# A fused two-block transformer kernel: the pool of feature tiles is allocated from the other end of the on-chip memory

## The chip, the cores and the metric

The kernel runs on one core of one Trainium2 chip. The core has a matrix engine (TensorE, PE in the profile; its weight loads are PEld), a vector engine (DVE), a scalar engine (ACT), a general engine (GpSimd, POOL), queues that issue transfers (SP and POOL here), 16 DMA engines, and two on-chip memories of 128 partitions: SBUF, which holds operands, and PSUM, into which TensorE accumulates. The metric is the device time of one execution in microseconds (us), as the median of several runs.

## The reference

The input is 512 tokens of width 1024, all in float32. A first block runs once: RMS norm, one projection `x @ w_in`, a recurrent mixer (RWKV-7) and a sparse attention (NSA) side by side, `h + y @ w_out`, RMS norm, and a gated feed-forward network of hidden width 2816:

```
def swiglu(x, w_gate, w_up, w_down):
    return (jax.nn.silu(x @ w_gate) * (x @ w_up)) @ w_down
```

A second block runs twice, with a layer norm ahead: a projection, a depthwise convolution, a differential attention with four heads and an attention to a memory of 256 tokens, an output projection, a layer norm, and a feed-forward network of hidden width 4096:

```
x = layer_norm(ALPHA * x + mixed, ln1_g[l], ln1_b[l])
ff = jnp.square(jax.nn.relu(x @ w_up[l])) @ w_down[l]
x = layer_norm(ALPHA * x + ff, ln2_g[l], ln2_b[l])
```

## The kernel before

Every large product is done in split precision. An operand is held as a high part (`xh`, `wh`, `hh`), rounded to TensorE's float32r, and a low part (`xl`, `wl`, `hl`), the rest. `mm3` (line 212) makes one product of a 128-row slice out of three matmuls: high by low, low by high, high by high, all into one PSUM tile (`acc`). In a matmul the first operand after the output is stationary (loaded into the array by a weight load), the second is moving (streamed through it, 512 columns, 256 in a few places). In a row of the profile, `acc<-xl,wh` names the moving operand first.

There are two shapes of large product.

- **Feature-major** (`fm_part`, line 230, and `fm_steps`, line 235): weights are stationary, features `X` are moving. One output tile of 128 features by 512 tokens takes 8 slices x 3 = 24 matmuls. It makes the gate and up products of both feed-forward networks and the projections at the start of the mixers. `gemm_fm_lead` (line 249) does the first four tiles of a stage in two halves of 256 tokens, so that they can begin before all tokens are ready.
- **Token-major** (`gemm_tm`, line 263): hidden activations (or mixer outputs) are stationary, weights are moving. It makes the down products and `w_out`.

```
def fm_part(ps, wt, X, t0, t1):
    wh, wl = wt
    for k in range(8):
        mm3(ps[:, t0:t1], wh[:, k, :], wl[:, k, :], *xk(X, k, slice(t0, t1)), k == 0, k == 7)
```

A weight tile of 512 KB arrives by DMA in `wraw` (or in halves of a feature tile, `raws`), ACT rounds it to `wh` (line 204) and DVE or POOL subtracts to get `wl` (line 208). The weights of the second block's mixers are split ahead of time during the feed-forward networks (`split_ahead`, line 152: `ahead` tiles, written back to HBM as `split`).

SBUF is divided into pools. `scope` (line 71) opens a pool; `side="right"` allocates it from the top of SBUF downwards, otherwise it is allocated from the bottom upwards, each pool behind the ones that are open. The pool of feature tiles, `xp` (line 78, name "x"), has 8 buffers of 8192 bytes a partition. It stays open for the whole kernel and holds `X`, the mixer outputs `y`, `qm`, `kt`, `vt2`, the memory's features `mh` and `ml`, `ahead` and `raws`. It is opened third of the SBUF pools, after `const` and `small`, so the pools that are opened later on the left lie above it. In the first stage the weights and several work pools are taken from the right (lines 369 to 372, and line 1119 for the first part of `w_out`); from line 1192 on the weight pool is on the left.

The order of instructions on each engine is set by a scheduler that works from the program's dependences, except where a stretch is pinned to the written order (`P["pin"]`).

Of the kernel before, what the change touches and what calls it, by code (L numbers as in the profile page):

```python
# [8 lines left out]
F32 = mybir.dt.float32  # L9
# [41 lines left out]
def tile_hybrid_blocks(ctx: ExitStack, tc: tile.TileContext, I, out):  # L51
# [19 lines left out]
    def scope(st, name, bufs=1, **kw):  # L71
        return st.enter_context(tc.tile_pool(name=name, bufs=bufs, reuse_waits="tile", **kw))
# [2 lines left out]
    small = ctx.enter_context(tc.tile_pool(name="small", bufs=8))  # L75
    wk = ctx.enter_context(tc.tile_pool(name="wk", bufs=1, space=PSUM))
    dram = ctx.enter_context(tc.tile_pool(name="dram", bufs=1, space=DRAM))
    xp = scope(ctx, "x", 8)

    ka = const.tile([128, 483], F32, name="ka")  # L80
    ident, mhalf, tri, hones = ka[:, 0:128], ka[:, 128:160], ka[:, 160:288], ka[:, 288:290]
# [1732 lines left out]
```

## Time and profile before

| | us |
|---|---|
| median of 3 runs (1955.12 to 1959.68) | 1959.52 |
| the profiled execution, whole | 1963.28 |
| its span, first to last instruction | 1961.3 |
| TensorE busy in the span | 1915.7 (98%) |
| DVE busy | 1132.1 (58%) |
| ACT busy | 782.9 (40%) |
| mean granted TensorE clock | 0.993 of full |

A busy TensorE is not the same as a TensorE at its peak: matmuls overlap, and their ends are modelled. What a stream of matmuls costs is read from the starts of successive ones in the timeline.

### The profile page before, as it was taken

What the parts mean: (1) busy time and instruction counts of PE and PEld (TensorE: products, weight loads), DVE (VectorE), ACT (ScalarE), POOL (GpSimd) and SP (SyncE); (2) the same over time, 40 slices, a digit from 0 to 9 for tenths busy, and PEclk for the clock granted to TensorE, in tenths of its full rate; (3) what the DMA queues carried; (4) which work ended last, traced back from release to release, by engine and by line L of the source; (5) the groups of instructions that cost most, each with busy time, mean ns of one, the idle gap of its engine ahead of it and who ended that gap; (6) DMA issues with size and microseconds to landing.
All of it is one profiled execution on the core that took longest, in us unless ns stands there. A gap on an engine that the chain in (4) does not pass through costs nothing.

```text
span 1961.3 us, 27788 instructions
## 1 busy us (share of the span) xinstructions
PE 1915.7 (98%) x10831; PEld 1583.3 (81%) x10831; DVE 1132.1 (58%) x1976; ACT 782.9 (40%) x1419; POOL 382.2 (19%) x450
## 2 busy tenths in 40 slices
PE   8999999999999999999999999999999999999998
PEld 7777777798888888978888888888978888888886
DVE  4674667665455535668766565545668764434345
ACT  4523565434434322356615444331357523223230
POOL 2211132223322101432112232100442010000000
PEclk9899999999999999999999999999999999999999
DMA  6147100458999922833448999732743433323331
GB/s 170 44 127 177 32 2 2 132 160 292 344 345 323 296 86 70 309 136 117 148 141 287 336 354 350 258 107 81 279 149 101 144 119 107 104 90 97 97 97 43
DMA packets 231591, 326.24 MB, mean 166 GB/s; under 512 B 29813, under 2 KB 157151, under 8 KB 231460
## 3 DMA queue, kind: packets, MB, share of 16 engines
q1 hardware_dynamic: 197636, 200.86, 33.2%
q0 software_dynamic: 33824, 123.62, 17.8%
q8 instruction: 85, 1.39, 0.3%
q14 instruction: 46, 0.38, 0.1%
HBM read 249.44 MB, written 77.09 MB: 166 GB/s over the span
## 4 chain that ended last, share of the span: by engine, by line
PE 88%; DVE 6%; ACT 2%; DMA 1%; issue 1%; POOL 1%; SPq 0%; DVEq 0%; ACTq 0%; POOLq 0%
PE acc L63 74%; PE ps_s L63 2%; PE ps_t L63 2%; PE ps_pt L63 1%; PE ps_po L63 1%; PE ps_pv L63 1%; PE ps_q L63 1%; DMA wraw<-in_w_in_dram 1%; PE ps_g L63 1%; PE ps_y L63 1%; PE ps_pm L63 1%; DVE e L1502 1%; ACT pr L1565 1%; DVE cv L1402 0%; PE ps_ptb L63 0%
## 5 line engine op out<-in xcount | busy, mean ns | idle before, releaser
L63 PE MATMUL acc<-xl,wh 128*128 128x512 f32 (+1 forms) x1432 | 529.1, 370 | 0.3 <-DVE xl L334 0.3
L63 PE MATMUL acc<-xh,wl 128*128 128x512 f32 (+1 forms) x1432 | 524.0, 366 | 0.7 <-DVE wl L208 0.6
L63 PE MATMUL acc<-xh,wh 128*128 128x512 f32 (+1 forms) x1432 | 523.1, 366 | 0.0
L63 PEld LDWEIGHTS acc<-xl,wh 128*128 128x128 f32 x1432 | 271.0, 189 | 52.9 <-issue 3.8
L63 PEld LDWEIGHTS acc<-xh,wh 128*128 128x128 f32 x1432 | 270.8, 189 | 48.2
L63 PEld LDWEIGHTS acc<-xh,wl 128*128 128x128 f32 x1432 | 270.7, 189 | 47.1 <-DVE wl L208 1.3
L63 PE MATMUL acc<-wh,hl 128*128 128x512 f32 x688 | 267.8, 389 | 0.0
L63 PE MATMUL acc<-wh,hh 128*128 128x512 f32 x688 | 266.8, 389 | 0.0
L63 PE MATMUL acc<-wl,hh 128*128 128x512 f32 x688 | 266.6, 390 | 0.0
L204 ACT CAST wh<-wraw 128x1024 fp32r<-128x1024 f32 (+2 forms) x123 | 126.2, 1028 | 215.0 <-PE acc L63 152.1
L208 DVE TENSOR_TENSOR wl<-wraw,wh 128x1024 fp32r<-128x1024 f32 (+2 forms) x119 | 142.7, 1200 | 90.0 <-ACT wh L204 89.7
L208 DVE TENSOR_TENSOR wl<-raws,wh 128x1024 fp32r<-128x1024 f32 (+1 forms) x92 | 111.3, 1213 | 134.5 <-ACT wh L204 134.5
L296 POOL TENSOR_TENSOR r<-v,ka 128x1 f32<-128x1 f32 (+1 forms) x40 | 41.0, 1026 | 666.0 <-DVE v L315 480.2
L204 ACT CAST wh<-raws 128x1024 fp32r<-128x1024 f32 (+1 forms) x92 | 94.9, 1035 | 153.3 <-PE acc L63 114.1
L63 PEld LDWEIGHTS acc<-wh,hl 128*128 128x128 f32 x688 | 129.2, 188 | 27.0
L63 PEld LDWEIGHTS acc<-wl,hh 128*128 128x128 f32 x688 | 129.1, 188 | 26.8
L63 PEld LDWEIGHTS acc<-wh,hh 128*128 128x128 f32 x688 | 129.2, 188 | 26.8
L1769 DVE TENSOR_TENSOR h<-h 128x512 f32<-128x512 f32 x64 | 44.3, 692 | 131.2 <-ACT h L1768 130.7
L170 DVE TENSOR_TENSOR ahead<-ahead 128x1024 fp32r<-128x1024 f32 x68 | 82.5, 1222 | 62.0 <-ACT ahead L169 61.9
L169 ACT CAST ahead<-ahead 128x1024 fp32r<-128x1024 f32 x68 | 71.1, 1050 | 92.7 <-DMA ahead<-in_w_in_dram 53.5
L1768 ACT ACTIVATE h<-acc 128x512 f32<-128x512 f32 x64 | 38.2, 597 | 171.9 <-PE acc L63 171.9
L1410 POOL TENSOR_TENSOR cv<-cv,cm 128x512 f32<-128x512 f32 x60 | 89.1, 1486 | 73.2 <-ACT cm L1407 69.5
(400 smaller groups left out, 2907.8 us busy)
## 6 DMA issues: line engine op xcount, KB each, us to landing
split<-ahead POOLq DMA_DIRECT2D x136, 512.0 KB, 6.9
wh<-split SPq DMA_DIRECT2D x68, 512.0 KB, 5.5
wl<-split SPq DMA_DIRECT2D x68, 512.0 KB
ahead<-in_w_in_dram POOLq DMA_DIRECT2D x36, 512.0 KB, 7.5
wraw<-in_w_down_dram SPq DMA_DIRECT2D x32, 512.0 KB, 3.7
raws<-in_w_down_dram SPq DMA_DIRECT2D x32, 512.0 KB
wraw<-in_w_up_dram SPq DMA_DIRECT2D x28, 512.0 KB, 5.3
raws<-in_w_up_dram SPq DMA_DIRECT2D x28, 512.0 KB
```

The lines of the kernel that those rows point to most:

```text
L63: i = getattr(self.eng, op)(*a, **k)
L169: act.copy(hi.bitcast(F32R), raw)
L170: dve.tensor_sub(raw.bitcast(F32R), raw, hi)
L204: act.copy(wh, raw)
L208: P["lo"].tensor_sub(wl[:, c], raw[:, c], wh[:, c].bitcast(F32))
L296: pool.tensor_tensor(o, v, mhalf[:, :n], op=OP.pow)
L1410: pool.tensor_add(cv[f], cv[f], m)
L1502: dve.tensor_tensor_reduce(e_, ps, W[:, 384 - 128 * qt:896 - 128 * qt], -0.125, 3e38, OP.add, OP.min, nm)
L1565: act.activation(pr[:, j, :], ps[:, j, :], AF.Exp, bias=nm[:, j:j + 1], scale=0.125, accum_out=u.sums[:, j, e:e + 1])
L1768: act.activation(h, ps, AF.Relu)
L1769: dve.tensor_mul(h, h, h)
```

## The change

```
     dram = ctx.enter_context(tc.tile_pool(name="dram", bufs=1, space=DRAM))
-    xp = scope(ctx, "x", 8)
+    scope(ctx, "gap", side="right").tile([128, 24], F32, name="gap")
+    xp = scope(ctx, "x", 8, side="right")
```

A tile of 24 floats (96 bytes a partition) that nothing reads or writes is taken from the top of SBUF, and the pool of features directly below it. The pools on the left start 65536 bytes lower, the other pools on the right 65632 bytes lower. In the built programs every engine has the same instructions in the same order, with the same waits on the same counts; only addresses differ. Byte offsets in a partition, as the two programs place the tiles:

| tiles | before | after | before mod 128 | after mod 128 |
|---|---|---|---|---|
| features (8 tiles of 8192) | 21056 to 86591 | 163712 to 229247 | 64 | 0 |
| weights `wh`, `wl`, from line 1192 on | 137856 to 178815 | 72320 to 113279 | 0 | 0 |
| weights `wraw`, from line 1192 on | 129664 to 137855 | 64128 to 72319 | 0 | 0 |
| hidden activations `hh`, `hl` | 178816 to 219775 | 113280 to 154239 | 0 | 0 |
| weights `wh`, `wl`, first stage, right | from 180192 | from 114560 | 96 | 0 |
| `w_out`'s first half, right | from 204768 | from 139136 | 96 | 0 |
| residual rows `tok` | from 86592 | from 21056 | 64 | 64 |
| tiles of line 1162 (`uc`, `W`, `cvh` and others) | from 102976 | from 37440 | 64 | 64 |
| `ks` of the first block | 108096 | 42560 | 64 | 64 |

Slices of these tiles that matmuls read begin at multiples of 512 bytes from a tile's start, so the remainders hold for them too (in `vtk_steps`, line 579, whose rows have 1120 bytes, every second slice is 96 bytes further).

## Rows read from the trace of the kernel before

**Rows 1.** The page, part 1 (busy us) and part 4 (the chain).
```profile
PE 1915.7 (98%) x10831; PEld 1583.3 (81%) x10831; DVE 1132.1 (58%) x1976; ACT 782.9 (40%) x1419; POOL 382.2 (19%) x450
...
PE 88%; DVE 6%; ACT 2%; DMA 1%; issue 1%; POOL 1%; SPq 0%; DVEq 0%; ACTq 0%; POOLq 0%
```

**Rows 2.** The chain in order of time, its longest pieces: start, us, what.
```profile
463.90 204.89 PE acc L63 x888
...
1028.24 253.94 PE acc L63 x1152
...
1608.35 345.11 PE acc L63 x1560
```

**Rows 3.** Busy time by stretch: engines in the header's order, then clock, DMA share.
```profile
core 0: us, PE busy (x) PEld busy (x) DVE busy (x) ACT busy (x) POOL busy (x), PEclk, DMA share, GB/s
50.00:100.00 50.00, 48.23 (x288) 36.58 (x288) 34.83 (x54) 26.46 (x41) 14.59 (x12) 0.90 0.15 43
...
440.00:640.00 200.00, 200.00 (x872) 162.21 (x871) 103.73 (x107) 84.92 (x98) 59.79 (x96) 1.00 0.96 326
...
840.00:1000.00 160.00, 153.68 (x840) 128.23 (x839) 111.52 (x281) 91.15 (x226) 39.35 (x34) 1.00 0.35 119
...
1060.00:1200.00 140.00, 140.00 (x613) 114.50 (x612) 77.36 (x81) 57.87 (x67) 42.21 (x67) 1.00 1.02 345
1620.00:1900.00 280.00, 280.00 (x1229) 228.41 (x1228) 113.84 (x131) 81.53 (x107) 0.00 (x0) 1.00 0.32 98
```

**Rows 4.** Timeline of PE, first feed-forward network, gate and up: starts 24 matmuls apart.
```profile
570.33 0.39 PE L63 MATMUL acc<-xl,wh 128*128 128x512 f32 x1
...
575.93 0.39 PE L63 MATMUL acc<-xl,wh 128*128 128x512 f32 x1
```

**Rows 5.** Timeline of PE, the same network's down product: starts 24 matmuls apart.
```profile
539.89 0.39 PE L63 MATMUL acc<-wl,hh 128*128 128x512 f32 x1
...
545.33 0.39 PE L63 MATMUL acc<-wl,hh 128*128 128x512 f32 x1
```

**Rows 6.** Timeline of PE, last feed-forward network, up: starts 24 matmuls apart.
```profile
1864.95 0.39 PE L63 MATMUL acc<-xl,wh 128*128 128x512 f32 x1
...
1870.55 0.39 PE L63 MATMUL acc<-xl,wh 128*128 128x512 f32 x1
```

**Rows 7.** Timeline of PE, w_out: weights on the right to 392.47, on the left after.
```profile
387.09 0.39 PE L63 MATMUL acc<-wl,yh 128*128 128x512 f32 x1
...
392.71 0.40 PE L63 MATMUL acc<-wl,yh 128*128 128x512 f32 x1
...
393.41 0.39 PE L63 MATMUL acc<-wl,yh 128*128 128x512 f32 x1
...
398.90 0.39 PE L63 MATMUL acc<-wl,yh 128*128 128x512 f32 x1
```

**Rows 8.** Groups by line and form: xcount, busy us, mean ns, idle before.
```profile
L63 PE MATMUL acc<-xl,wh 128*128 128x512 f32 x1048 | 419.9, 401 | 0.0
...
L208 DVE TENSOR_TENSOR wl<-wraw,wh 128x1024 fp32r<-128x1024 f32 x113 | 138.3, 1225 | 84.3 <-ACT wh L204 84.0
...
L208 DVE TENSOR_TENSOR wl<-raws,wh 128x1024 fp32r<-128x1024 f32 x90 | 110.0, 1224 | 131.3 <-ACT wh L204 131.3
L63 PE MATMUL acc<-xl,wh 128*128 128x256 f32 x384 | 109.2, 286 | 0.3 <-DVE xl L334 0.3
```

**Rows 9.** Timeline of PE, half tiles: before the first network; memory's keys, first layer.
```profile
423.20 0.28 PE L63 MATMUL acc<-xh,wh 128*128 128x256 f32 x1
...
426.02 0.28 PE L63 MATMUL acc<-xh,wh 128*128 128x256 f32 x1
...
812.90 0.28 PE L63 MATMUL acc<-ml,wh 128*128 128x256 f32 x1
...
815.62 0.28 PE L63 MATMUL acc<-ml,wh 128*128 128x256 f32 x1
```

**Rows 10.** Waits, 1620 to 1900 us, then 1060 to 1200: total us, times, longest.
```profile
ACT wh L204 <- PE acc L63: 102.2, 24, 8.5
...
ACT wh L204 <- PE acc L63: 17.1, 9, 5.3
```

## The prediction

> **What bounds the kernel now.** I read the page first, then the chain of waits, then the busy time by stretch, then single matmuls in the timeline. TensorE is busy 98% of the span, and 88% of the chain that ends last is TensorE [rows 1]. The long pieces of the chain are unbroken TensorE work: 204.89, 253.94 and 345.11 us [rows 2], in all 804 us. In the feed-forward stretches TensorE is busy 200.00 of 200, 140.00 of 140 and 280.00 of 280 us, at a granted clock of 1.00 (2.4 GHz) [rows 3]. So there only what a matmul costs from start to start counts, and a change that touches no instruction can matter only through that. The durations in the rows (0.39 us) overlap; the cost is the distance between starts.
>
> **The instructions.** Every engine has the same instructions in the same order, with the same waits. The gap tile is read and written by nothing: 0 us. So there is no wait to add or remove and no queue that anything is moved past. What changes is addresses.
>
> **What an address costs TensorE.** The gate and up products run 24 matmuls in 575.93 - 570.33 = 5.60 us, 233.3 ns each [rows 4]. The down product, also of 512 columns, at the same granted clock and with TensorE never idle, runs 24 in 545.33 - 539.89 = 5.44 us, 226.7 ns each [rows 5]. The difference is 6.67 ns for a matmul. Three things differ between the two: which operand is moving (features there, weights here), how many matmuls follow each other into one PSUM tile (24 or 6), and where the moving operand begins (64 bytes past a multiple of 128, or on one).
>
> One product separates these. `w_out` runs with the same stationary operand and in the same order, first with weights on the right, 96 bytes past a multiple of 128, then with weights on the left, on one: 24 matmuls in 392.71 - 387.09 = 5.62 us (234.2 ns), then in 398.90 - 393.41 = 5.49 us (228.8 ns) [rows 7]. Role and grouping are unchanged, only the moving address changed, and 5.4 ns of the 6.7 went. The 2.1 ns that remain above 226.7 go with a stationary operand (`yh`, `yl`) that still begins at remainder 64. I take the rule from this: a 512-column matmul costs 226.7 ns where both operands begin on a multiple of 128 bytes, 6.7 ns more where the moving one does not, some 2 ns more where only the stationary one does not. It is a reading of four streams, not a known law.
>
> The trace differs here from the notes. The Trainium skill, page "TensorE: Matmul & The Clock Gate", section "Back-to-back issue gap", gives N / 2.4 + 2.5 ns, 215.8 for 512 columns, with no term for an address; by it the two streams would run alike and the sum would be 0. The page "SBUF — State Buffer" of the Trainium skill, section "Specifications (TRN2)", gives lines of 16 bytes; 21056 and 163712 are both multiples of 16, so by it too the sum would be 0.
>
> After the change the features begin at remainder 0, and the weights and hidden activations keep it.
>
> **The sum.** There are 3 x 1048 = 3144 matmuls of 512 columns with features moving [rows 8].
> - Feed-forward networks: the first has 22 tiles for gate and 22 for up, less 4 that run in halves: 40 x 24 = 960. The other two have 28 each outside the halves: 56 x 24 = 1344. The memory queries `qm` add 4 x 24 = 96. These 2400 stand in unbroken TensorE work: 2400 x 6.67 ns = 16.0 us, all on the path.
> - The heads' projections: 16 x 24 = 384, inside the mixers, where TensorE is busy 153.68 of 160 us [rows 3] and its gaps wait for DVE and ACT. Worth 0 to 2.6 us; I take half, 1.3.
> - The first stage: the remaining 360, 0 to 2.4 us. Here a stretch shows 48.23 busy of 50 us at a clock of 0.90 [rows 3]; I take half, 1.2.
> - Half tiles: 3 x 384 = 1152 matmuls of 256 columns [rows 8]. Before the first network they cost (426.02 - 423.20) / 24 = 117.5 ns, but the memory's keys, also at remainder 64, cost (815.62 - 812.90) / 24 = 113.3 ns [rows 9]. So at this width two rates occur at the same remainder and the rule is not enough. Bounds: 0 and 1152 x 4.2 ns = 4.8 us; I take 2, as some already run at the lower rate.
> - Stationary operands in the pool: 96 matmuls of `w_out` with weights on the right go from 234.2 to 226.7 ns, 0.7 us; another 480 (96 of `w_out`, 192 of `v_steps`, 192 of the second block's `w_out` with `y`) lose 2.1 ns, 1.0 us. Part lies in the mixers: 1.2 of 1.7.
> - Scores with `kt` moving: 128 x 6.67 ns, 0 to 0.85 us; 0.4.
> - DVE and ACT: subtractions from `raws` (remainder 64) take 1224 ns, from `wraw` (remainder 0) 1225 ns [rows 8]: 0.
>
> Together 16.0 + 1.3 + 1.2 + 2 + 1.2 + 0.4 = 22.1 us, between 16.0 and 28.4. The profiled execution took 1963.28 us, so it would take 1941.2. It lay 3.8 us above the median of the runs, 1959.52; I take the difference over to the median: 1937.4, say **1937**, with 1931 to 1943.5 as the bounds, and 2 us at each side for runs that spread over 4.6 us.
>
> **What keeps the gain from being seen elsewhere.** Faster up products ask for weights 3% sooner. In the last network ACT waits 102.2 us for TensorE to free a weight buffer [rows 10], with a DMA share of 0.32 [rows 3]: supply is far ahead.
>
> **Rivals.**
> - *Transfers become the bound.* From 440 to 640 and from 1060 to 1200 us the DMA engines are at 0.96 and 1.02 of their time [rows 3], loading weights and moving the `ahead` tiles. If these stretches kept their length, at most their 872 + 613 matmuls x 6.67 ns = 9.9 us would be lost: 1947. For it: there is no DMA time left. Against it: TensorE does not wait there now, ACT still waits for TensorE [rows 10], and the `ahead` work can end later.
> - *The rate belongs to the product, not to the address.* Then nothing changes: 1959.5. For it: the grouping into PSUM differs too, and the half tiles show two rates at one remainder [rows 9]. Against it: `w_out` [rows 7]. The two pages' rules give this time as well.
> - *Slower: the rate belongs to the region.* Moving operands between 21056 and 86591, and those from 204768 on, are the slow ones; the weights at 137856 to 178815 are the fast ones. After the change the weights lie at 72320 to 113279 and most features above 180000. If place decides, the features stay slow and the down products (86 slices x 8 x 3 = 2064 matmuls) go to 233.3 ns: +13.8 us, 1973. It decides from the point where the down product's 24 starts take 5.60 us. Against it: in the last network a quarter of the moving operands are in the tile at 78400, and the rate is the same 233.3 ns as with tiles at 21056 to 53823 [rows 4, 6]; the region would need two borders that happen to follow the remainder.
> - *The change does not do what it says.* The addresses above are the built program's, so I give this nothing.
>
> **How the numbers follow.** The forecast 0.74, transfers 0.08, no change 0.11, slower by region 0.06, and 0.01 for another gain. A difference below 0.3% (5.9 us) can't be told from none. Faster by more: 0.74 + 0.08 + 0.01 = 0.83; within: 0.11; slower: 0.06. The range 1929 to 1947 takes in the forecast's bounds with the spread of runs and the case of transfers, about 0.8.
>
> **What would show it.** In the timeline of after, 24 starts of the up products 5.44 us apart instead of 5.60 in all three networks, the down products still 5.44, and both halves of `w_out` at 5.44 to 5.46. The long pieces of the chain shorten by the count of their up matmuls times 6.67 ns, and mixers by little. Up products that stay at 5.60 us make the prediction wrong as a whole; 5.44 there with new TensorE waits for `wl` or `wraw` would be the transfers; down products at 5.60 would be the region.

## The result, and the profile after

The changed kernel took 1947.43 us (median of 4 runs, 1945.12 to 1948.87), the kernel before 1959.60; the ratio is 0.9937, 95% interval 0.9917 to 0.9956. The sign was right, the size was not: 12.2 us where 22.5 had been forecast, and 0.4 us outside the range. Measured a second time, later, the same kernel took 1944.23 against 1959.47: 0.9916 (0.9904 to 0.9928), 15.2 us.

The page of the changed kernel, its parts 1 and 4, reads almost as in [rows 1]:

```profile
PE 1899.4 (98%) x10831; PEld 1587.9 (82%) x10831; DVE 1131.4 (58%) x1976; ACT 783.3 (40%) x1419; POOL 382.4 (20%) x450
...
PE 87%; DVE 7%; ACT 3%; issue 1%; DMA 1%; POOL 1%; SPq 0%; DVEq 0%; POOLq 0%; ACTq 0%
```

The count of matmuls is the same; the busy time of TensorE fell by 16.3 us, and that of DVE, ACT and POOL moved by less than 1 us. The long pieces of the chain (start, us, what) answer to [rows 2]:

```profile
461.92 201.38 PE acc L63 x888
...
1021.43 251.00 PE acc L63 x1152
...
1597.17 340.83 PE acc L63 x1560
```

They are 3.5, 2.9 and 4.3 us shorter, with the same number of matmuls in each. The timeline of TensorE shows where that comes from: starts 24 matmuls apart, first in the down product of the first network, then in its gate and up products [rows 5, 4].

```profile
535.74 0.39 PE L63 MATMUL acc<-wh,hh 128*128 128x512 f32 x1
...
541.18 0.39 PE L63 MATMUL acc<-wh,hh 128*128 128x512 f32 x1
...
564.98 0.39 PE L63 MATMUL acc<-xh,wh 128*128 128x512 f32 x1
...
570.42 0.39 PE L63 MATMUL acc<-xh,wh 128*128 128x512 f32 x1
```

Both take 5.44 us. Before, the down product took 5.44 and the up products 5.60. `w_out`, weights on the right and then on the left [rows 7]:

```profile
384.81 0.39 PE L63 MATMUL acc<-wh,yh 128*128 128x512 f32 x1
...
390.26 0.39 PE L63 MATMUL acc<-wh,yh 128*128 128x512 f32 x1
...
392.30 0.39 PE L63 MATMUL acc<-wh,yh 128*128 128x512 f32 x1
...
397.74 0.39 PE L63 MATMUL acc<-wh,yh 128*128 128x512 f32 x1
```

They take 5.45 and 5.44 us instead of 5.62 and 5.49. So every stream of 512 columns that the prediction named runs as it said. The half tiles of 256 columns do not; before the first network:

```profile
421.28 0.28 PE L63 MATMUL acc<-xl,wh 128*128 128x256 f32 x1
...
424.16 0.28 PE L63 MATMUL acc<-xl,wh 128*128 128x256 f32 x1
```

24 of them take 2.88 us, 120.0 ns each, more than either rate of before, 117.5 and 113.3 [rows 9]. They became slower in every stretch from 417 us on. Only the 192 of the first stage kept their time, because they had taken 120.0 ns before the change too (start, us, what, starts 24 matmuls apart in the kernel before):

```profile
31.05 0.28 PE L63 MATMUL acc<-xl,wh 128*128 128x256 f32 x1
...
33.93 0.28 PE L63 MATMUL acc<-xl,wh 128*128 128x256 f32 x1
```

Transfers took nothing back: busy time by stretch, where the DMA engines are full [rows 3].

```profile
core 0: us, PE busy (x) PEld busy (x) DVE busy (x) ACT busy (x) POOL busy (x), PEclk, DMA share, GB/s
...
440.00:640.00 200.00, 200.00 (x884) 165.50 (x883) 104.24 (x106) 84.22 (x97) 61.78 (x98) 1.00 0.97 332
...
1060.00:1200.00 140.00, 140.00 (x619) 115.78 (x618) 80.34 (x85) 60.31 (x70) 42.49 (x68) 1.00 1.03 352
```

In the same time TensorE does 884 and 619 matmuls instead of 872 and 613, still without a gap, and the DMA engines move 332 and 352 GB/s instead of 326 and 345.

Since both kernels have the same instructions in the same order on TensorE, the distance from each start to the next can be subtracted, matmul by matmul. These are the sums over the two profiled executions:

| matmuls | count | gain, us | the prediction's term |
|---|---|---|---|
| 512 columns, features moving | 3144 | 19.85 | 16.0 + 1.3 + 1.2 = 18.5 |
| 256 columns, features moving | 1152 | -2.94 | +2 |
| 256 columns, memory's keys and values | 192 | -0.85 | none |
| `w_out`, `v_steps`, `cvh` (stationary in the pool, or beside it) | 864 | -0.16 | 1.2 |
| down products | 2063 | 0.15 | 0 |
| scores with `kt` moving | 128 | 0.50 | 0.4 |
| all other | 3287 | -0.98 | 0 |
| sum | | 15.56 | 22.1 |

Of the 19.85 us in the first row, 1.5 are not the address. They come from the one tile of the first stage that runs behind the small `ps_x` matmuls: in the execution of before TensorE's granted clock was 0.54 over the 3.5 us shown, so at its lower level of 1.2 GHz for most of them, and starts lay 0.43 us apart; in the execution of after, behind the same small matmuls, it was 1.00 (the engines' busy time and instructions in the order of [rows 3], then clock, DMA share and GB/s; before, then after):

```profile
187.50:191.00 3.50, 3.50 (x13) 2.70 (x10) 0.43 (x2) 0.93 (x2) 1.31 (x3) 0.54 0.35 136
```

```profile
186.50:190.00 3.50, 3.50 (x21) 2.86 (x16) 0.43 (x2) 1.15 (x2) 1.64 (x3) 1.00 0.12 43
```

So 18.3 us are left for the address at 512 columns.

### The profile page after: what moved, and what is told of

Read it like the earlier page. It is cut to its first block, busy times and chain, and to the rows that moved or that the text cites. A ratio compares the mean times of both kernels' runs of the same rounds, so it can differ in the third digit from the quotient of the medians.

```text
span 1945.9 us, 27788 instructions
## 1 busy us (share of the span) xinstructions
PE 1899.4 (98%) x10831; PEld 1587.9 (82%) x10831; DVE 1131.4 (58%) x1976; ACT 783.3 (40%) x1419; POOL 382.4 (20%) x450
## 4 chain that ended last, share of the span: by engine, by line
PE 87%; DVE 7%; ACT 3%; issue 1%; DMA 1%; POOL 1%; SPq 0%; DVEq 0%; POOLq 0%; ACTq 0%
PE acc L63 73%; PE ps_s L63 2%; PE ps_t L63 2%; PE ps_pt L63 1%; PE ps_pv L63 1%; PE ps_po L63 1%; DVE e L1503 1%; PE ps_g L63 1%; PE ps_q L63 1%; PE ps_y L63 1%; PE ps_pm L63 1%; DMA wraw<-in_w_in_dram 1%; ACT pr L1566 1%; DVE cv L1403 1%; POOL r L297 0%
```

## The experiments

Up to here the rule of the prediction (the moving operand's own remainder modulo 128) holds for 512 columns and is silent on 256. The first three runs were made to try that rule against its rival, the place in SBUF.

**The features aligned, but left where they were.** A gap of 64 bytes below the pool and one above it:

```
+    scope(ctx, "gap").tile([128, 16], F32, name="gap")
     xp = scope(ctx, "x", 8)
+    scope(ctx, "gap2").tile([128, 16], F32, name="gap2")
```

> The features stay at their old place on the left; a tile of 64 bytes below them and one above move them to remainder 0 of 128 (21120 on), and everything above them by 128 bytes, so that no other remainder changes. Theory A, the remainder decides: 24 up matmuls of 512 columns take 5.44 us as in the changed kernel, the half tiles of 256 columns 120.0 ns a matmul, and the whole takes the changed kernel's time, 1947.4 us, within 3. Theory B, the place in SBUF decides: 5.60 us, half tiles at 113 to 118 ns, 1959.5 us within 3.

Measured: 1961.96 us against 1960.56, ratio 1.0009 (0.9999 to 1.0019). TensorE's timeline in the last network's up products, starts 24 matmuls apart:

```profile
1860.19 0.39 PE L63 MATMUL acc<-xl,wh 128*128 128x512 f32 x1
...
1865.79 0.39 PE L63 MATMUL acc<-xl,wh 128*128 128x512 f32 x1
```

5.60 us, as before the change, though the features now begin on a multiple of 128 bytes, like the weights. The rule of the prediction is false. The half tiles from 408 us on took 118.3 to 120.1 ns, mostly 118.4 to 119.0, which neither theory had expected.

**The features moved, but not aligned.** The change with a gap of 32 bytes instead of 96:

```
-    scope(ctx, "gap", side="right").tile([128, 24], F32, name="gap")
+    scope(ctx, "gap", side="right").tile([128, 8], F32, name="gap")
```

> The pool of features on the right as in the changed kernel, but below a gap of 32 bytes instead of 96, so that it begins at 163776, remainder 64 as before; the first stage's weights go to remainder 64 with it. Theory A, the remainder decides: 24 up matmuls take 5.60 us, the half tiles 113.3 or 117.8 ns a matmul, 1959.5 us within 3. Theory B, the place decides: 5.44 us, and 1947.4 us within 3.

Measured: 1949.96 us, ratio 0.9947 (0.9931 to 0.9964), with the features at remainder 64. The same timeline:

```profile
1852.93 0.39 PE L63 MATMUL acc<-xh,wl 128*128 128x512 f32 x1
...
1858.42 0.39 PE L63 MATMUL acc<-xh,wl 128*128 128x512 f32 x1
```

5.49 us, 228.8 ns a matmul: neither 5.44 nor 5.60. Both runs spoke for the place against the remainder, but that value did not fit it, and in this kernel `w_out` with weights on the left had become slower than before (233.2 ns instead of 228.8).

**Streams by themselves**, for 16 pairs of remainders.

> No product of the reference: only streams of matmuls in the order of the three-matmul product, 48 of them for each pair of remainders (moving, stationary) out of 0, 32, 64 and 96 at 512 and at 256 columns, on constant data, output zeros. A letter stands for a remainder: a is 0, b 32, c 64, d 96, e 16; the first letter is the moving operand's. Theory A, remainders alone decide: 512 columns 226.7 ns at a_a, 233.3 at c_a and c_d, 228 to 230 at a_c; 256 columns 120.0 at a_a and c_d, 113.3 or 117.8 at c_a and a_c. If only the difference of the two remainders counted, a_a, b_b, c_c and d_d would be equal at either width, and a_c equal to c_a. If it is something else in the kernel (transfers, evictions of PSUM), the streams, which have neither, all take the same time, 226.7 or less at 512 columns and 113.3 at 256.

First rows of neighbouring streams of 48 matmuls, from the timeline:

```profile
60.86 0.39 PE L47 MATMUL full_a_a<-xl,wh 128*128 128x512 f32 x1
71.95 0.39 PE L47 MATMUL full_a_b<-xl,wh 128*128 128x512 f32 x1
83.04 0.40 PE L47 MATMUL full_a_c<-xl,wh 128*128 128x512 f32 x1
94.23 0.39 PE L47 MATMUL full_a_d<-xl,wh 128*128 128x512 f32 x1
```

(71.95 - 60.86) / 48 = 231.0 ns with both operands at remainder 0, where 226.7 was expected; `full_c_c` took 231.0 too, `full_a_c` 233.1. So the streams do differ with nothing else running, and not by one operand's remainder. The run, a single execution, settles no more than that: its tiles were 16512 and 4224 bytes long, so `xl` began 128 bytes further than `xh` modulo 256, and `wl` than `wh`, and every stream mixed two cases.

That flaw gave the next theory. If the cost depends on the distance from the moving operand to the stationary one modulo 256, all rates seen so far fall into line: 0 in the down products of every kernel and in the changed kernel's up products (226.7 ns), 64 in the up products before (233.3), 128 with the features aligned in place (233.3), 192 with the gap of 32 bytes (228.8). `w_out` before has 96 with weights on the right (234.2) and 192 with weights on the left (228.8).

**Streams by distance.** All four tiles begin alike modulo 256; 16 distances at two widths, and some of them with both operands shifted.

> No product of the reference: only streams of 48 matmuls in the order of the three-matmul product, on constant data, output zeros. All four operand tiles begin alike modulo 256, and a stream's letter says how far, modulo 256, the stationary operand begins behind the moving one, in steps of 16 bytes (a 0, e 64, i 128, m 192). The streams called moved (and movedhalf) shift both operands by 64, 128 and 192 (first letter) at distances 0, 64, 128 and 192 (second letter). Theory C, formed from the first runs: a matmul's cost depends on that distance modulo 256 and on nothing else of the addresses. It expects at 512 columns 226.7 ns at 0, 233 at 64 and 128, 229 at 192, the same in the shifted streams; at 256 columns 120.0 at 0, 113.3 or 117.8 at 64, 118 to 120 at 128, 117.8 at 192. Theory B, the place in SBUF: all streams lie close together, so no stream differs from another of its width. Theory A, each operand's own remainder modulo 128: a and i alike, and streams shifted by 64 unlike those that aren't.

The first rows of some streams, from the timeline; a stream's matmul costs the distance to the next stream's first row, divided by 48:

```profile
59.67 0.39 PE L47 MATMUL full_a<-xl,wh 128*128 128x512 f32 x1
70.55 0.39 PE L47 MATMUL full_b<-xl,wh 128*128 128x512 f32 x1
...
103.83 0.39 PE L47 MATMUL full_e<-xl,wh 128*128 128x512 f32 x1
115.02 0.39 PE L47 MATMUL full_f<-xl,wh 128*128 128x512 f32 x1
...
148.58 0.40 PE L47 MATMUL full_i<-xl,wh 128*128 128x512 f32 x1
159.78 0.39 PE L47 MATMUL full_j<-xl,wh 128*128 128x512 f32 x1
...
193.21 0.39 PE L47 MATMUL full_m<-xl,wh 128*128 128x512 f32 x1
204.20 0.40 PE L47 MATMUL full_n<-xl,wh 128*128 128x512 f32 x1
...
237.50 0.28 PE L47 MATMUL half_a<-xl,wh 128*128 128x256 f32 x1
243.25 0.28 PE L47 MATMUL half_b<-xl,wh 128*128 128x256 f32 x1
...
260.26 0.28 PE L47 MATMUL half_e<-xl,wh 128*128 128x256 f32 x1
265.71 0.28 PE L47 MATMUL half_f<-xl,wh 128*128 128x256 f32 x1
```

| distance, bytes mod 256 | 0 | 16 | 32 | 48 | 64 | 80 | 96 | 112 |
|---|---|---|---|---|---|---|---|---|
| 512 columns, ns | 226.7 | 226.9 | 233.1 | 233.3 | 233.1 | 231.7 | 234.2 | 233.3 |
| 256 columns, ns | 119.8 | 118.3 | 118.3 | 117.7 | 113.5 | 118.5 | 119.0 | 119.8 |

| distance, bytes mod 256 | 128 | 144 | 160 | 176 | 192 | 208 | 224 | 240 |
|---|---|---|---|---|---|---|---|---|
| 512 columns, ns | 233.3 | 233.3 | 233.3 | 229.8 | 229.0 | 233.3 | 233.3 | 227.1 |
| 256 columns, ns | 118.5 | 120.0 | 120.0 | 118.1 | 113.5 | 116.7 | 116.7 | 119.6 |

At 512 columns the theory's four values come out, and shifting both operands by 64, 128 or 192 bytes leaves them within 1 ns. At 256 columns 0 is one of the dearest distances, and 64 and 192 are the cheapest, at 113.5, where 117.8 had been expected at 192; with both operands shifted by 64, 128 or 192 bytes these two ran at 117.8, while three repeats of the unshifted stream at 64, at the end of the run, took 113.7 again. So at distances 64 and 192 a stream of 256 columns has two rates, as the kernel before already showed at distance 64 [rows 9], and the theory's second half, that nothing else of the addresses counts, is false at this width.

Nor does the table give the time of the run before it, matmul by matmul. There the three matmuls of a product have different distances, and the mean of their values in the table is right for `full_a_a` (distances 128, 128, 0: 231.1, measured 231.0) but not for `full_a_c` (192, 192, 64: 230.4, measured 233.1). The table is shown for streams in which all matmuls have one distance, as in the large products of the kernel.

The Trainium skill, page "TensorE: Matmul & The Clock Gate", section "Back-to-back issue gap", has N / 2.4 + 2.5 ns, 215.8 at 512 columns, for a matmul by itself. No stream here reaches it: the least is 226.7, and the distance between the operands, which the formula doesn't have, adds up to 7.5 ns.

**In the kernel: place against distance.** Two kernels in which the theories say the opposite. First the features moved and at remainder 0 of 128, but at distance 128 (a gap of 224 bytes):

```
-    scope(ctx, "gap", side="right").tile([128, 24], F32, name="gap")
+    scope(ctx, "gap", side="right").tile([128, 56], F32, name="gap")
```

> The pool of features on the right as in the changed kernel, below a gap of 224 bytes: it begins at 163584, remainder 0 of 128 as in the changed kernel, but from the moving features to the stationary weights (72320 on) the distance is 128 modulo 256 instead of 0. Theory C, the distance: up matmuls of 512 columns at 233 ns, half tiles at 118 to 120, the first stage alone at the lower rate (its weights move along, distance 0); about 1959 us, within 3. Theory B, the place: 226.7 to 229 ns and 1947 to 1950 us.

Measured: 1959.61 us, ratio 0.9997 (0.9988 to 1.0006): the whole gain is gone. Up products of the last network, 5.60 us for 24:

```profile
1864.69 0.39 PE L63 MATMUL acc<-xl,wh 128*128 128x512 f32 x1
...
1870.29 0.39 PE L63 MATMUL acc<-xl,wh 128*128 128x512 f32 x1
```

Then the features at their old place at distance 0 (64 bytes below the pool, 192 above):

```
+    scope(ctx, "gap").tile([128, 16], F32, name="gap")
     xp = scope(ctx, "x", 8)
+    scope(ctx, "gap2").tile([128, 48], F32, name="gap2")
```

> The features stay on the left (21120 on), 64 bytes are put below them and 192 above, so that the distance to the weights from line 1192 on (138112 on) is 0 modulo 256. Theory C, the distance: up matmuls 226.7 ns, half tiles 120.0, as in the changed kernel but for the first stage (distance 96, 234 ns): 1948 to 1952 us. Theory B, the place: 233.3 ns and 1959 to 1962 us, as in the run with 64 bytes on either side.

Measured: 1945.34 us, ratio 0.9919 (0.9905 to 0.9932), below the range of the expectation, and 5.44 us for 24:

```profile
1855.14 0.39 PE L63 MATMUL acc<-xl,wh 128*128 128x512 f32 x1
...
1860.58 0.39 PE L63 MATMUL acc<-xl,wh 128*128 128x512 f32 x1
```

The gain needs no move to the other end; 256 bytes of gaps do it. With that the place is out, and at 512 columns the distance is shown to set the rate. By what mechanism it does, no run here shows.

**The change once more.**

> The changed kernel once more, in the same rounds as the kernel before. If the spread of single runs follows the granted clock of the first stage, the ratio holds, 0.993 to 0.995 at equal clocks, and the time goes down with the mean clock by about 1.3 us for 0.001.

Measured: 1944.23 us, ratio 0.9916. Its granted clocks were 0.993 to 0.997, those of the first measurement 0.994 to 0.995. The profiled executions show where the clock differs, in the stretch from 60 to 120 us (TensorE busy and matmuls, clock, DMA share, GB/s), first in the first measurement, then in this one:

```profile
60.00:120.00 60.00, 57.01 (x356) 0.91 0.25 66
```

```profile
60.00:120.00 60.00, 55.92 (x372) 1.00 0.31 75
```

The same kernel, the same stretch of the first stage: at a clock of 0.91 it did 356 matmuls, at 1.00 372, and the two spans are 1945.9 and 1940.0 us. In the 104 runs of these kernels whose mean clock is known, one slope fitted for all falls by 1.56 us for each 0.001 of it (1.00 is 2.4 GHz). Brought to a clock of 0.995, the kernel before takes 1960.3 us (43 runs, standard error 0.2) and the changed one 1946.0 and 1945.5 (0.5 each). At equal clock the change is worth 14.3 to 14.8 us, a ratio of 0.9925 to 0.9927, just under the 0.993 to 0.995 expected. The kernel with gaps of 64 and 192 bytes is at 1946.6 by the same slope, 0.6 to 1.1 us above the changed one; its first stage ran at 234 ns in the median, the changed kernel's at 227.

**The half tiles at distance 64, all else at 0.** Weight tiles are made 256 bytes longer, and those of the half tiles and of the memory's products begin 64 bytes in (`P["off"]` is 16 around them, `P["pad"]` 64 from line 1192 on); the memory's values, where the weights are moving, come to 192 by this. The room comes from smaller buffers in the second block's mixers (`"e": 4`, `"jk": 1`).

```
+    def w_tile(n, a, b):
+        o = P["off"] if P["pad"] else 0
+        t = P["w"].tile([128, a * b + P["pad"]], F32R, name=n, tag=n)
+        return t[:, o:o + a * b].rearrange("p (a b) -> p a b", a=a)
```

> The changed kernel, in which the weight tiles from line 1192 on are 256 bytes longer and those of the half tiles and of the memory's keys and values begin 64 bytes into theirs, so that these 256-column products run at distance 64 and all others still at 0. To make room, the second block's mixers have four buffers for e instead of five and one for jk instead of two. Theory C, the distance: 960 matmuls with features moving and 192 with the memory's go from 120.0 ns to 113.3 or 117.8, 2.5 to 7.7 us less than the changed kernel's 1944.2 in its second measurement, 1936.5 to 1941.7, unless the smaller buffers cost something in the mixers. Its rival, that 256 columns are slow for a reason that only goes along with the distance (the shorter time for a weight load): they stay at 120 ns, and 1944 us or more.

Measured: 1942.66 us, ratio 0.9906 (0.9891 to 0.9921). Two of its stretches of half tiles, 24 matmuls each:

```profile
423.62 0.28 PE L63 MATMUL acc<-xl,wh 128*128 128x256 f32 x1
...
426.45 0.28 PE L63 MATMUL acc<-xh,wh 128*128 128x256 f32 x1
...
1014.86 0.28 PE L63 MATMUL acc<-xl,wh 128*128 128x256 f32 x1
...
1017.58 0.28 PE L63 MATMUL acc<-xl,wh 128*128 128x256 f32 x1
```

The first takes 2.83 / 24 = 117.9 ns, the second 2.72 / 24 = 113.3. So both rates occur again at one distance. The time is 1.0 us above the expected range.

> As the run before it, with two buffers for the mixers' l tiles instead of three, in place of four for e. The same 113.3 or 117.8 ns in the half tiles; 1936.5 to 1941.7 us if the smaller buffers cost nothing.

Measured: 1945.98 us, ratio 0.9921 (0.9906 to 0.9937), at a low mean clock (0.9935); 1943.4 brought to 0.995, above the expected range either way. The half tiles run at 113.3 to 118.0 ns.

The control, the first of these with the half tiles' weights at offset 0 again:

> The first of these three (four buffers for e, one for jk, weight tiles 256 bytes longer), with the half tiles' weights at the beginning of their tiles: distance 0 for all. It shows what the smaller buffers cost by themselves: half tiles at 120.0 ns, and the changed kernel's 1944.2 us plus that cost.

Measured: 1944.38 us, ratio 0.9914 (0.9899 to 0.9930), half tiles at 120.0 ns:

```profile
421.80 0.28 PE L63 MATMUL acc<-xl,wh 128*128 128x256 f32 x1
...
424.68 0.28 PE L63 MATMUL acc<-xh,wh 128*128 128x256 f32 x1
```

(2.88 us for 24 starts.) So the smaller buffers cost nothing that shows, and the offset brings 1.7 us between the medians, 2.9 at equal clock (1941.9 against 1944.8). In the traces the 256-column matmuls after 380 us take 135.86 us in all instead of 139.28, 3.4 less. The version is the fastest of all here, by an amount that the ratios' intervals don't separate from the changed kernel.

## Why the prediction was wrong

**What held.** In the feed-forward stretches TensorE alone sets the time; waits and transfers don't enter. The 512-column term, 18.5 us, measured 18.3 without the 1.5 that a tile gained by the clock. Within it, the first stage gave 0.9 us where 1.2 had been taken (2.38 with that tile, which would have looked like all of its 2.4), and the mixers 2.29 where 1.3 and the 0.6 of `qm` had. The up products went to 5.44 us, the down products stayed there, and no new wait for weights came up.

**The step that failed: the rule taken from `w_out`.** The prediction said that in `w_out` "only the moving address changed", and put the difference down to the moving operand's remainder modulo 128 [rows 7]. But when one operand moves, its distance to the other changes too: 96 modulo 256 in the first half, 192 in the second. The runs showed that the distance decides at 512 columns and the remainder alone does nothing: remainder 0 at distance 128 brought no gain in two kernels, one at each end of SBUF. The forecast of the 512-column streams came right because this change happens to bring the distance from 64 to 0. The same four streams allowed both readings, and the prediction called its own "a reading of four streams"; the table of addresses had what was needed to tell that a second variable moved along.

**The term that this spoiled: the half tiles.** They were taken at +2 us, between 0 and 4.8, from a rule for 512 columns and two rates in [rows 9]. They measured -2.94, and the memory's products, left out of the sum, -0.85: together 5.8 us of the 6.5 by which the sum of 22.1 missed 15.56. At 256 columns the order of the distances is another: 0 costs 120.0 ns, 64 costs 113.3 or 117.8. No row of before showed a 256-column stream after line 1192 at distance 0, and a bound that excludes a loss had no reason behind it. That this width can cost 120.0 ns stood in the trace of before, in the first stage at 31 us.

**The small terms.** Stationary operands in the pool (1.2) came to nothing on the path: -0.16. In the stretches without gaps `w_out` and its kin did gain 0.8 us, and the waits of the mixers took it back. `kt` gave 0.50 where 0.4 had been taken, and all other matmuls lost 0.98. The 1.5 us of the clock make up for part of these, by luck: without them the sum would be 14.1 us.

**From the execution to the median.** The profiled execution lay 3.8 us above the median of three runs, and the prediction carried that difference over. After the change it was 0.45. The difference goes with the clock of the first stage in a single execution (a mean of 0.993 there, 0.995 over the 43 runs), not with the kernel, so 3.3 us of the miss of 10.4 come from this step, 6.5 from the terms above, and the rest is rounding.

**The rivals.** Transfers: not bound, as [rows 3] and the rows of after show. That the rate belongs to the product: out, since `w_out` and the up products followed the addresses. The region: it looked right after two runs and fell with the next pair, and in none of these kernels did the down products leave 226.7 ns.

What stays open is why the distance counts at all, and why a stream of 256 columns at distance 64 or 192 takes one rate or the other. In the streams by themselves a shift of both operands went with the slower one. In the kernel the addresses are the same modulo 256, and yet the rate holds through many tiles and then changes, between stretches and now and then within one: in the kernel before, the memory's keys ran at 113.3 ns in the first layer [rows 9] and at 117.8 in the second. Nothing run here chose it.

## What to carry to other kernels

Where TensorE is never idle, compare the start-to-start distance of matmuls of one width over the whole kernel; if streams of the same shape differ, tabulate the difference of the two operands' addresses modulo 256, not each address, and try a gap of some bytes. On this kernel a distance of 0 is best at 512 columns and 64 or 192 at 256, so the two widths want different offsets. A price read off a natural experiment in a trace needs the list of everything that changed along with it, and a width that wasn't seen needs a bound on both sides of zero.

## What the runs showed of the hardware

- In a stream whose matmuls all have one distance, from the moving to the stationary operand in bytes modulo 256, a 512-column matmul costs 226.7 to 234.2 ns by that distance. Where the two tiles lie in SBUF made no difference above 1 ns. Streams of mixed distances do not take the mean.
- A 256-column matmul costs 113.3 to 120.0 ns. The distance doesn't settle it by itself: two rates, 113.3 and 117.8 ns, occur at one distance in the same execution.
- The granted clock from 60 to 120 us was 0.91 in one execution of the changed kernel and 1.00 in another, with the span 5.9 us shorter. In the profiled execution of the kernel before it was 0.54 from 187.5 to 191 us, and one tile lost 1.5 us by it. Over 43 runs of the kernel before, the time and the mean clock go together with a correlation of -0.82.
